# A Hymba-style layer on one core: token chunks of 272, 384, 384 instead of 352, 344, 344, and a reordered first stage

## The chip, the core and the metric

The kernel runs on one core of one Trainium2 chip. The metric is device time in microseconds (us). The core has a matrix engine (TensorE, PE in the profile, with its weight loads shown apart as PEld), a vector engine (VectorE, DVE), an activation engine (ScalarE, ACT), a general one (GpSimd, POOL) and a queue engine (SyncE, SP). Each works through its own instructions in order. DMAs are issued here from SP and from POOL.

## The reference

One decoder layer on 1024 tokens of width 1024, float32, with 16 learned meta tokens set in front, so 1040 rows in all. The parts, each with a residual and an RMSNorm ahead of it:

```
h = h + 1/2 * SwiGLU_1(RMSNorm(h))          # 1024 -> 2 x 2816 -> 1024
u = RMSNorm(h) @ W_in                       # 1024 -> 3584
o = concat[ HGRN2(u_hgrn), StickBreaking(u_sb) ]
h = h + o @ W_out
h = h + 1/2 * SwiGLU_2(RMSNorm(h))
swiglu(h) = (silu(h @ w_gate) * (h @ w_up)) @ w_out
```

HGRN2 is a gated linear recurrence with 4 heads of 128, stick-breaking attention has 8 heads of 64. The meta tokens are dropped at the end.

## The kernel before, in words

Every product is made of three matmuls on rounded float32 operands: each operand is split into a high part, cast by ACT, and a low part, the rest, made by a DVE subtraction; high x high, low x high and high x low are summed in PSUM (`times`, lines 316 to 323, order wh.xh, wl.xh, wh.xl).

The tokens of the first feed-forward layer are cut into three chunks, `THIRDS` (line 29): chunk 0 with n0 columns, chunks 1 and 2 with nw columns each. Chunk 0 is multiplied plainly. Chunks 1 and 2 go together through a Strassen-like scheme: with the pair of chunks as one side and two halves of the inner dimension as the other, seven block products stand in for eight. The operands of the seven products are called B11, B21, B22, T1, T2, T3, T4 and are sums and differences of the normalized chunks; `first_block` (line 665) turns a chunk's rows into columns on PE and evicts them, `first_combined` (line 681) makes the sums.

**First stage, gate and up projections** (`fast_in`, line 262). The 2816 hidden features are 22 tiles of 128, for gate and for up. It opens with chunk 0 alone: `plain_quad` (line 332) multiplies 256 features of gate or up, 48 matmuls, with four weight blocks of 256 KB (`block`, line 282: a ring called `raw`, 6 buffers, loaded from SP). Six such calls are made ahead, for six feature tiles of gate and of up. They are the time in which the rows of chunks 2 and 1 are normalized (`norm_rows`, line 638), turned and combined. Then come 22 quads (`quad`, line 339) of 84 matmuls on the pair of chunks; the last 16 of them carry also chunk 0, 48 matmuls more, with the same weights. `operand` (line 275) splits a weight block, 512 columns, in three buffers each for the high and the low part. Results go to DRAM from POOL's queue (`act1D`).

**Order in the opening** (lines 1378 to 1397). PE's order is as written by hand; the other engines' order is found by the compiler's list scheduler from the order of writing, the priorities and estimated times. Written order: all row loads (chunk 0 from SP in line 1364, chunks 2 and 1 from POOL in line 1365, nine buffers of 4 KB per partition); norm and turning of chunk 0; plain call 1; norm of chunk 2; plain call 2; norm of chunk 1; turning of chunk 2; plain calls 3 and 4; turning of chunk 1; then calls 5 and 6 with four steps of `first_combined` ahead of each; the other twelve steps; the 22 quads.

**Second stage, down projection** (`fast_out`, line 489). `plain_round` (line 544) does chunk 0 for all 22 hidden tiles f: 24 matmuls for each f, from two weight blocks of 256 KB (`raw`, line 504) and one activation tile (`right`, line 509). Both rings have `ring_bufs` buffers, 5 so far; the split parts have four buffers each (`halved`, line 514), which is two f for the weights. Behind the matmuls of f = 3 the residual `hT`, eight loads of 520 KB, is written into SP's order (`load_h`). It waits until the memory under it is free. Then seven steps follow (A12, A11, S1, S2, S4, S3, A22), each of 11 rounds of 12 matmuls, for the pair of chunks. `A11` loads 11 weight blocks of 256 KB into a place of their own (`ak`, line 527), so that these loads have no ring to wait for. The norm of the next layer is woven in between (`norm_steps`, by chunk).

After that: the projections for the mixer (`project`, `project_early` and `hgrn_fill`; the keys, values and gates of all 1040 rows go by `THIRDS`, 16 column tiles of 24 matmuls for each chunk, the rest by halves of 512), the two kinds of heads woven together (`weave`, `braid`: lists of steps with estimated costs, 0.42 ns per column and 13 ns per matmul), the output projection, and the second feed-forward layer with two chunks of 512, all Strassen.

Memory for a stage's tiles is stacked by pool. The first stage's pools are, from the bottom: the operands (X for chunk 0, then B11, B21, B22, T1, T2, T3, T4), then `w1` (raw, wh, wl, s), then the small ones. The second stage puts from the same bottom: `xh` and `xl` (33,280 bytes per partition each), the norm's tiles, `hT` (33,280 bytes), then `sk` and `ak`.

Of the kernel before, what the change touches and what calls it, by code (L numbers as in the profile page):

```python
# [11 lines left out]
F32 = mybir.dt.float32  # L12
# [3 lines left out]
AF = mybir.ActivationFunctionType  # L16
# [4 lines left out]
P = 128  # L21
D = 1024
# [5 lines left out]
EPS = 1e-6  # L28
THIRDS = [(0, 352), (352, 344), (696, 344)]
HALVES = [(META, 512), (META + 512, 512)]  # L30
# [9 lines left out]
class Block:  # L40
# [221 lines left out]
    def fast_in(self, ops, n, w_in, actD, openers, ev0, open_ev, feed=None, plain=None,  # L262
# [6 lines left out]
        nc = self.nc  # L269
        wp, pin = self.wq, self.pin  # L270
# [11 lines left out]
        def block(i, h, col):  # L282
            t = wp.tile([P, 4, P], F32, tag="raw", name="raw", bufs=6)
            nc.sync.dma_start(
                t, w_in[512 * h : 512 * h + 512, col + P * i : col + P * i + P]
                .rearrange("(k p) f -> p k f", p=P)
            )
            return t
# [200 lines left out]
    def fast_out(self, hT, cs, n, w_out, actD, load_h, ready, between=lambda a, q: None,  # L489
# [4 lines left out]
        nc = self.nc  # L494
        op, ring, pout = self.op, self.ring, self.pout
# [8 lines left out]
        def raw(i, j, q):  # L504
            t = ring.tile([P, 512], F32, tag="raw", name="raw", bufs=self.ring_bufs)
            nc.sync.dma_start(t, block(i, j, q))
            return t

        def right(key, n):
            t = ring.tile([P, n], F32, tag="act", name="act", bufs=self.ring_bufs)  # L510
            nc.sync.dma_start(t, actD[key])
            return t
# [125 lines left out]
    def norm_rows(self, ci, rows, junk):  # L638

        nc = self.nc  # L640
        for i, (row, at, m) in enumerate(rows):
# [5 lines left out]
            else:  # L647
                nc.scalar.activation(junk[0][:m], row[:m], AF.Square, accum_out=s)
            nc.scalar.activation(r, s, AF.Sqrt, bias=self.eps[:m], scale=1.0 / D)
            nc.vector.reciprocal(r, r)  # L650
# [675 lines left out]
    def run(self):  # L1326
        nc, tc, a = self.nc, self.tc, self.a
# [19 lines left out]
        with ExitStack() as c0:  # L1347
            with ExitStack() as c1:
                with tc.manual_schedule(engines={nc.tensor.engine}), ExitStack() as c2:
# [8 lines left out]
                    self.pin = self.pool("pin1", 1, PSUM, c2)  # L1358
                    self.t_bufs = 2
                    c3 = ExitStack()  # L1360
                    rp = self.pool("rows", ctx=c3, side="right")
                    junk = [rp.tile([P, D], (BF16, U8)[i], name=f"junk{i}") for i in range(2)]
                    self.row_bufs = 9
                    rows = [self.rows_of(0, rp, nc.sync)]
                    rows += [self.rows_of(ci, rp, nc.gpsimd) for ci in (2, 1)]
                    turning = []
# [14 lines left out]
                    with tc.high_priority():  # L1381
                        self.first_plain(rows[0], junk, plain)
                    next(steps)
                    self.norm_rows(2, rows[1], junk)
                    next(steps)
                    self.norm_rows(1, rows[2], junk)
                    ba = self.first_block(2, rows[1], rp, "ba", ops)
                    next(steps)
                    next(steps)
                    bb = self.first_block(1, rows[2], rp, "bb", None)  # L1390
                    made = self.first_combined(ba, bb, ops, rp, nw)
                    for _ in range(2):
                        for _ in range(4):
                            next(made)
                        next(steps)
# [6 lines left out]
                with tc.manual_schedule(engines={nc.tensor.engine}), ExitStack() as c2:  # L1402
# [8 lines left out]
                    hT = ph.tile([P, KT, T], F32, name="hT")  # L1411
                    self.ring_bufs = 5
                    early_w = []
# [155 lines left out]
            with tc.manual_schedule(engines={nc.tensor.engine}), ExitStack() as cx:  # L1569
# [71 lines left out]
                self.pin = self.pool("pin2", 1, PSUM, cx)  # L1641
                self.t_bufs = 2
                ppb = self.pool("ppb", 1, PSUM, pre)
# [18 lines left out]
            with tc.manual_schedule(engines={nc.tensor.engine}), ExitStack() as c1:  # L1662
# [16 lines left out]

                self.ring_bufs = 6  # L1680
                self.fast_out(hT, (cA, cB), n, a["ffn2_w_out"][0], actD, load_h, ready)
# [23 lines left out]
```

## Time and profile before

| | |
|---|---|
| median of 3 runs (lowest, highest) | 2140.38 us (2135.32, 2140.86) |
| the profiled execution's own time | 2136.56 us |
| its span, first to last instruction | 2134.9 us |
| PE busy | 2049.6 us, 96% |
| DVE busy | 1358.4 us, 64% |
| ACT busy | 899.1 us, 42% |
| POOL busy | 673.5 us, 32% |

Reading it: a row of the timeline gives start and length in us, engine, line, operation, output tile, input tiles, shape and how many were merged; the bracket is the idle time of the engine ahead of it and what ended it. A row with a q behind the engine's name is an instruction of the queue, so a DMA's issue. A table by windows gives for each stretch the busy time of each engine with the number of instructions, the granted clock, the share of time of the 16 DMA engines and the rate. Matmuls overlap, so a matmul's own length (the mean in a table of groups) is longer than the distance from one start to the next; how long a chain takes is read from that distance.

### The profile page before, as it was taken

To read this page: it belongs to the slowest core of one execution; us is meant where nothing else is said; L and a number is where in the kernel's file an instruction comes from. 1 tells how busy PE (TensorE), PEld (TensorE's weight loads), DVE (VectorE), ACT (ScalarE), POOL (GpSimd) and SP (SyncE) were. 2 spreads that over 40 slices of the span, in tenths; PEclk is the share of its full clock that TensorE was granted. 3 is DMA by queue.
4 is the path that set the end of the run, shared out by engine and by line. 5 is a ranking of instruction groups with operands and counts; after the bars stand their busy time and mean duration, and the time that the engine had idled before them with its cause. 6 is when DMAs were issued, how large, how long until landed. Compare 5 with 4: busy or idle time off the path is not lost. (4 is left out here: it accounts for less than half of the span.)

```text
span 2134.9 us, 32078 instructions
## 1 busy us (share of the span) xinstructions
PE 2049.6 (96%) x11520; PEld 1841.8 (86%) x11520; DVE 1358.4 (64%) x2072; ACT 899.1 (42%) x1859; POOL 673.5 (32%) x732
## 2 busy tenths in 40 slices
PE   6899999999999999999999999999899999999998
PEld 6899999999999989988887878877688888878887
DVE  5775544555589843246666757658767677676774
ACT  7543333333465633455565623335223333234443
POOL 2265544452000322333443400112545454440000
PEclk9999999999999999999999999999999999999999
DMA  6543333324867735434444171334533333358363
GB/s 178 163 153 118 121 105 102 103 92 174 263 197 227 228 93 160 145 129 114 117 138 113 59 262 49 97 114 123 173 104 109 94 109 99 104 180 278 104 202 133
DMA packets 271311, 300.19 MB, mean 141 GB/s; under 512 B 24784, under 2 KB 197904, under 8 KB 271152
## 3 DMA queue, kind: packets, MB, share of 16 engines
q1 hardware_dynamic: 252656, 244.88, 38.0%
q0 software_dynamic: 17456, 53.26, 6.8%
q8 instruction: 91, 1.49, 0.3%
q14 instruction: 68, 0.56, 0.1%
q10 hardware_dynamic: 1040, 0.00, 0.0%
HBM read 215.96 MB, written 82.11 MB: 140 GB/s over the span
## 5 line engine op out<-in xcount | busy, mean ns | idle before, releaser
L320 PE MATMUL qb<-T,wh 128*128 128x344 f32 (+1 forms) x1056 | 312.4, 358 | 11.0 <-DVE u L362 7.1
L279 DVE TENSOR_TENSOR wl<-s,wh 128x512 fp32r<-128x512 f32 x176 | 203.5, 1157 | 115.1 <-ACT wh L277 112.2
L320 PEld LDWEIGHTS qb<-T,wh 128*128 128x128 f32 x1056 | 194.0, 190 | 36.0 <-ACT wh L277 8.8
L588 PE MATMUL o<-tl,wh 128*128 128x344 f32 (+1 forms) x616 | 219.2, 357 | 3.4 <-DVE tl L518 3.3
L588 PE MATMUL o<-th,wh 128*128 128x344 f32 (+1 forms) x616 | 219.2, 357 | 3.3 <-DVE hT L598 3.3
L588 PE MATMUL o<-th,wl 128*128 128x344 f32 (+1 forms) x616 | 218.9, 357 | 0.7 <-DVE wl L518 0.7
L320 PE MATMUL qa<-B,wh 128*128 128x344 f32 (+1 forms) x704 | 210.4, 363 | 0.0
L163 PE MATMUL proj<-xh,wh 128*128 128x344 f32 (+2 forms) x576 | 208.0, 361 | 0.9 <-ACT xh L1443 0.9
L277 ACT CAST wh<-s 128x512 fp32r<-128x512 f32 x176 | 109.4, 622 | 225.9 <-PE qb L320 158.3
L279 DVE TENSOR_TENSOR wl<-raw,wh 128x512 fp32r<-128x512 f32 x172 | 151.0, 881 | 81.1 <-ACT wh L277 77.5
L164 PE MATMUL proj<-xh,wl 128*128 128x344 f32 (+2 forms) x576 | 202.1, 351 | 0.0
L165 PE MATMUL proj<-xl,wh 128*128 128x344 f32 (+2 forms) x576 | 201.7, 350 | 0.2 <-POOL xl L1444 0.2
L277 ACT CAST wh<-raw 128x512 fp32r<-128x512 f32 x172 | 106.0, 620 | 200.7 <-PE qc L320 98.3
L320 PE MATMUL qb<-T,wl 128*128 128x344 f32 (+1 forms) x528 | 188.8, 358 | 0.0
L320 PE MATMUL qd<-X,wh 128*128 128x352 f32 x704 | 181.2, 325 | 0.7 <-DVE X L661 0.7
L516 ACT CAST th<-act 128x512 fp32r<-128x512 f32 (+2 forms) x176 | 95.3, 542 | 183.0 <-PE o L588 129.9
L292 POOL TENSOR_TENSOR s<-raw 128x512 f32<-128x512 f32 x88 | 120.5, 1370 | 103.7 <-DVE wl L279 69.8
L518 DVE TENSOR_TENSOR tl<-act,th 128x512 fp32r<-128x512 f32 (+2 forms) x176 | 109.9, 627 | 67.0 <-ACT th L516 66.9
L320 PEld LDWEIGHTS qa<-B,wh 128*128 128x128 f32 x704 | 129.6, 190 | 16.1
L1212 POOL TENSOR_TENSOR sig<-sig,keep 128x144 f32<-128x144 f32 (+3 forms) x64 | 92.0, 1437 | 146.2 <-DVE keep L1209 86.2
L588 PEld LDWEIGHTS o<-tl,wh 128*128 128x128 f32 x616 | 117.0, 190 | 17.1 <-DVE tl L518 4.8
L320 PE MATMUL qa<-B,wl 128*128 128x344 f32 (+1 forms) x352 | 127.0, 361 | 3.9 <-DVE wl L279 3.9
(332 smaller groups left out, 4916.8 us busy)
## 6 DMA issues: line engine op xcount, KB each, us to landing
raw<-in_ffn_w_in_dram SPq DMA_DIRECT2D x208, 256.0 KB, 3.1
raw<-in_ffn_w_out_dram SPq DMA_DIRECT2D x176, 256.0 KB, 4.0
raw<-in_w_in_dram SPq DMA_DIRECT2D x28, 512.0 KB, 4.2
ks<-kD SPq DMA_DIRECT2D x32, 260.0 KB, 5.3
ak<-in_ffn_w_out_dram SPq DMA_DIRECT2D x22, 256.0 KB, 4.6
hT<-xD SPq DMA_DIRECT2D x8, 520.0 KB, 8.7
xD<-xts POOLq DMA_DIRECT2D x16, 256.0 KB, 2.8
vD<-vhl SPq DMA_DIRECT2D x8, 512.0 KB, 4.7
```

What stands on the lines that cost most here:

```text
L163: nc.tensor.matmul(ps, wh[:, s], xs, start=k == 0, stop=False)
L164: nc.tensor.matmul(ps, wl[:, s], xs, start=False, stop=False)
L165: nc.tensor.matmul(ps, wh[:, s], xl[:, k, c0 : c0 + n], start=False, stop=k == nk - 1)
L277: nc.scalar.copy(hi, src)
L279: nc.vector.tensor_sub(lo, src, hi.bitcast(F32))
L292: op(t, x, y)
L320: nc.tensor.matmul(ps, a[:, k, :], b[:, k0 + k, :], start=start and k == 0 and i == 0, stop=k == 3 and i == 2, skip_group_check=True,)
L516: nc.scalar.copy(hi, src)
L518: nc.vector.tensor_sub(lo, src, hi.bitcast(F32))
L588: nc.tensor.matmul(banks[bank][m], y[:, m * P : (m + 1) * P], z, start=start and q == 0 and e == 0, stop=q == nq - 1 and e == 2, skip_grou ...
L1212: nc.gpsimd.tensor_mul(sig, sig, keep[:, 1 : nk + 1])
```

## The change

Four things, all in the first feed-forward layer:

1. The chunks are 272, 384, 384 columns.
2. The rows of chunks 2 and 1 are loaded from SP, not POOL, and are written into the order where they are needed: chunk 2 behind the second plain call, chunk 1 behind the third. The rows have 7 buffers, not 9. The weight ring of the first stage has 7 buffers, not 6.
3. The norm keeps its last square root of chunk 0 as `self.root`, and the first plain call is written inside `issue_after(self.root.ins)`: instructions of that call on ACT are placed behind that square root.
4. Plain calls 1 and 2 stand ahead of the norm and turning of chunk 2, call 3 ahead of the load, norm and turning of chunk 1, and calls 4, 5 and 6 follow, each behind four steps of `first_combined`; eight steps are left for the end.

And the activation ring of the second stage has 4 buffers, not 5 (`ring_bufs` is a pair now: weights, activations). The last layer keeps 6 and 6.

```diff
-THIRDS = [(0, 352), (352, 344), (696, 344)]
+THIRDS = ((0, 272), (272, 384), (656, 384))
...
-            t = wp.tile([P, 4, P], F32, tag="raw", name="raw", bufs=6)
+            t = wp.tile([P, 4, P], F32, tag="raw", name="raw", bufs=self.in_bufs)
...
-            t = ring.tile([P, 512], F32, tag="raw", name="raw", bufs=self.ring_bufs)
+            t = ring.tile([P, 512], F32, tag="raw", name="raw", bufs=self.ring_bufs[0])
...
-            t = ring.tile([P, n], F32, tag="act", name="act", bufs=self.ring_bufs)
+            t = ring.tile([P, n], F32, tag="act", name="act", bufs=self.ring_bufs[1])
...
-            nc.scalar.activation(r, s, AF.Sqrt, bias=self.eps[:m], scale=1.0 / D)
+            self.root = nc.scalar.activation(
+                r, s, AF.Sqrt, bias=self.eps[:m], scale=1.0 / D
+            )
...
-                    self.t_bufs = 2
+                    self.t_bufs, self.in_bufs = 2, 7
...
-                    self.row_bufs = 9
+                    self.row_bufs = 7
                     rows = [self.rows_of(0, rp, nc.sync)]
-                    rows += [self.rows_of(ci, rp, nc.gpsimd) for ci in (2, 1)]
...
                     with tc.high_priority():
                         self.first_plain(rows[0], junk, plain)
+                    with tc.issue_after(self.root.ins):
+                        next(steps)
                     next(steps)
+                    rows.append(self.rows_of(2, rp, nc.sync))
                     self.norm_rows(2, rows[1], junk)
-                    next(steps)
-                    self.norm_rows(1, rows[2], junk)
                     ba = self.first_block(2, rows[1], rp, "ba", ops)
                     next(steps)
-                    next(steps)
+                    rows.append(self.rows_of(1, rp, nc.sync))
+                    self.norm_rows(1, rows[2], junk)
                     bb = self.first_block(1, rows[2], rp, "bb", None)
                     made = self.first_combined(ba, bb, ops, rp, nw)
-                    for _ in range(2):
+                    for _ in range(3):
                         for _ in range(4):
                             next(made)
                         next(steps)
...
-                    self.ring_bufs = 5
+                    self.ring_bufs = 5, 4
```

More of the change, by code (lines that the diff above doesn't have):

```diff
@@ L1641, in run @@
                 self.pin = self.pool("pin2", 1, PSUM, cx)
-                self.t_bufs = 2
+                self.t_bufs, self.in_bufs = 2, 6
                 ppb = self.pool("ppb", 1, PSUM, pre)
@@ L1678, in load_h @@
                             nc.sync.dma_start(hT[:, m, c : c + n], self.h2D[m, :, c : c + n])
-                self.ring_bufs = 6
+                self.ring_bufs = 6, 6
                 self.fast_out(hT, (cA, cB), n, a["ffn2_w_out"][0], actD, load_h, ready)
```

## The prediction

> **What bounds the kernel now.** First the page, for whose time it is:
>
> ```profile
> span 2134.9 us, 32078 instructions
> PE 2049.6 (96%) x11520; PEld 1841.8 (86%) x11520; DVE 1358.4 (64%) x2072; ACT 899.1 (42%) x1859; POOL 673.5 (32%) x732
> ```
>
> PE is the bound on the average, so the change is worth what it takes off PE's work and off PE's waits. Where the waits are is in the table by windows:
>
> ```profile
> core 0: us, PE busy (x) PEld busy (x) DVE busy (x) ACT busy (x) POOL busy (x), PEclk, DMA share, GB/s
> 0.00:20.00 20.00, 3.65 (x16) 3.27 (x16) 5.57 (x17) 6.79 (x13) 5.54 (x14) 1.00 0.95 282
> 20.00:40.00 20.00, 18.80 (x106) 18.20 (x107) 16.42 (x48) 19.46 (x36) 4.24 (x7) 1.00 0.56 126
> 60.00:80.00 20.00, 18.28 (x118) 17.26 (x117) 19.62 (x38) 15.46 (x36) 4.43 (x4) 1.00 0.39 110
> 80.00:100.00 20.00, 16.29 (x87) 16.00 (x86) 12.77 (x21) 6.75 (x13) 6.72 (x7) 0.83 0.63 192
> ...
> 22.00:84.00 62.00, 54.87 (x337) 52.48 (x337) 50.59 (x118) 50.90 (x102) 13.31 (x20) 1.00 0.44 119
> ...
> 540.00:560.00 20.00, 20.00 (x128) 20.00 (x127) 9.55 (x16) 8.76 (x16) 0.00 (x0) 1.00 0.99 339
> ...
> 1700.00:1720.00 20.00, 20.00 (x89) 16.38 (x88) 13.57 (x16) 5.24 (x9) 9.90 (x11) 1.00 0.34 106
> ...
> 940.00:1240.00 300.00, 286.14 (x1763) 246.44 (x1763) 199.42 (x269) 179.34 (x456) 117.92 (x146) 0.97 0.39 107
> ```
>
> In the first 20 us PE works 3.65 us while the DMA engines are full. From 20 to 84 us ACT and DVE are nearly as busy as PE (50.9 and 50.6 of 62 us), and DVE is full at the end of it. At 80 us there is a stall, and the granted clock falls to 0.83 in that window. From 540 on PE is full, and so is the DMA. Then the timeline of the opening, for what releases PE:
>
> ```profile
> 1.44 3.37 POOL L608 DMA_DIRECT2D row<-in_x_dram  x6
> 2.66 18.44 SPq L284 DMA_DIRECT2D raw<-in_ffn_w_in_dram  x9
> 9.31 3.65 PE L631 MATMUL xps<-ident,row 128*128 128x128 f32 x16 [9.31 <-DVE ss_x L650]
> 9.88 1.06 ACT L648 ACTIVATE junk<-row 96x1024 bf16<-96x1024 f32 x1 [1.01 <-DMA row<-in_x_dram]
> 16.32 0.62 ACT L277 CAST wh<-raw 128x512 fp32r<-128x512 f32 x1 [5.29 <-DMA raw<-in_ffn_w_in_dram]
> 16.84 0.29 ACT L649 ACTIVATE ss_x<-ss_x,eps 96x1 f32<-96x1 f32 x1
> 20.16 1.54 PE L631 MATMUL xps<-ident,row 96*128 96x96 f32 x8 [7.20 <-DVE row L651]
> 20.62 3.66 ACT L660 ACTIVATE X<-xps,g 128x352 fp32r<-128x352 f32 x8
> 22.40 0.66 PE L320 MATMUL qd<-X,wh 128*128 128x352 f32 x1 [0.70 <-DVE X L661]
> 84.53 0.66 PE L320 MATMUL qa<-B,wl 128*128 128x344 f32 x1 [3.71 <-DVE wl L279]
> ```
>
> The third row tile's square root (16.84) stands on ACT behind a weight cast (16.32) that waits 5.29 us for its block; that block was issued at 2.66 and shared the DMA with six row loads from POOL. PE waits 7.20 us for it. The first real matmul is at 22.40, the first quad gets going at 84.53.
>
> **The change: PE's work.** Distances from start to start come from full windows: 20 us / 126 = 0.159 us for 352 columns (128 records less two cut at the edges), 20 / 88 = 0.227 for 512. That is 0.0128 us + 0.42 ns per column. It gives 0.126 for 272, 0.157 for 344, 0.174 for 384. Does it hold as low as 272? The nearest rows are 264 wide, in the mixer:
>
> ```profile
> 992.45 0.28 PE L1199 MATMUL z<-ks,qs 128*128 128x264 f32 x1
> 992.57 0.28 PE L1200 MATMUL z<-ks,qs 128*128 128x264 f32 x1
> 992.70 0.28 PE L1140 MATMUL oacc<-wu,v 128*128 128x256 f32 x1
> ```
>
> They start 0.12 and 0.13 apart, so it does. Counts, from the loops: at n0 44 x 24 = 1056 in the first stage, 22 x 24 = 528 in the plain round, 16 x 24 = 384 projections, 1968 in all; at nw 22 x 84 = 1848, 7 x 11 x 12 = 924 and 768, 3540 in all. Change: 1968 x (-33.5 ns) + 3540 x (+16.8 ns) = -65.9 + 59.3 = -6.6 us. Of this, the opening's 288 matmuls give -9.6; all that follows gives +3.0 (the plain round -17.7, the seven steps +15.5, the rest +5.2).
>
> **The start.** Row loads from POOL are gone from the front (six issues, 3.37 us, off POOL; six on SP, at most as long by that row, behind weight loads that are not yet wanted). Chunk 0 is now 128 + 128 + 16 rows. Taking the rows' arrival as before at worst, row tile 2 comes by 9.9, its square 1.06 and its root 0.3 end by 11.5, and its scaling by 12.5. PE turns the first two tiles until 12.96, as now, then the third by about 13.2. From the first X eviction to the first matmul it took 22.40 - 20.62 = 1.8 us. So PE starts at 14 to 15 (13 if the rows come sooner); I take 14. The first cast no longer stands in front of the root, and with 3 MB less ahead of it its block is there.
>
> **The opening until the first quad.** PE's own work is 288 x 0.126 = 36.3 plus two turnings of about 4.5 and a cold start of 1: the first quad could come at 61. But DVE has 50.6 us of work between 22 and 84. What its widths do:
>
> ```profile
> L279 DVE TENSOR_TENSOR wl<-raw,wh 128x512 fp32r<-128x512 f32 x24 | 16.0, 689 | 6.9 <-ACT wh L277 6.7
> ...
> L223 DVE TENSOR_TENSOR T<-bb,T 128x344 fp32r<-128x344 f32 x4 | 1.8, 509 | 0.0
> ```
>
> (689 - 509) / 168 = 1.07 ns per column: 44 operations that widen by 40 columns cost +1.9 us, 14 that narrow by 80 save 1.2. So 51.3 us of DVE, and ACT the same. Packed as tightly as in 60 to 80 (0.98) it ends 52.3 us after 14, at 66; packed as loosely as over the whole (0.82) at 77. The combining starts a call earlier, and eight of its steps, not twelve, are left behind the last call, which makes for the tighter end. I take 72: 12.5 us sooner than 84.53, bounds 7.5 and 18. Of it 9.6 is the narrower matmul, the rest is the start. The first quad still starts out of a wait, with a cold clock as now. The loads: chunk 2's rows are behind eight weight blocks, of which the eighth waits for the first's buffer, free by about 13; they land by 19 at the 282 GB/s of the first window and are wanted by 27. Chunk 1's stand behind four more blocks, out at about 20, landed by 26, wanted by 37: hidden.
>
> **One queue or two.** The first weight cast waited until 16.32 for a block issued at 2.66. The Trainium skill, "DMA: Bandwidth & Descriptors", section "Issuing engines are not separate DMA queues", says that DMAs of all issuing engines share the same 16 engines and interleave, and that a second issuing engine saves only issue time. By that rule moving loads to SP buys nothing in rate; what can gain is the order, and the trace agrees: the blocks were issued early and landed after the rows.
>
> **The plain round** shrinks from 84 to 67 us, and the loads in it don't:
>
> ```profile
> 513.36 3.91 SPq L1418 DMA_DIRECT2D hT<-xD  x8
> 517.38 15.36 SPq L506 DMA_DIRECT2D raw<-in_ffn_w_out_dram  x6
> 531.71 0.43 PE L554 MATMUL o<-th,wh 128*128 128x352 f32 x1 [0.81 <-ACT wh L516]
> 532.43 0.43 PE L554 MATMUL o<-th,wl 128*128 128x352 f32 x1 [0.29 <-DVE wl L518]
> ```
>
> and, from the waits of SP's queue:
>
> ```profile
> SPq L1418 <- PE qd L320: 5.9, 1, 5.9
> ```
>
> The eight loads of 520 KB wait for PE's last matmul of the first stage, so PE begins the round as they are issued. The weights behind them are split and used 18.3 us later, at 531.71. Until then PE lives on the 4.5 f in hand (five buffers and four split ones, two for each f: 4.5 x 24 x 0.159 = 17.2 us), then waits 0.81 and 0.29 us. At 272 columns 4.5 f last 13.6 us. What saves it, if anything, is memory: `hT` ends, from the bottom, at 66,560 + 16,192 + 33,280 = 116,032 bytes now, inside wh, which PE reads to the end (weights begin at 99,584, six raw blocks end at 111,872). After, it ends at 117,312, and seven raw blocks end at 117,760, so of what PE reads it needs only T3 and T4, and T4 is done 12 x (0.126 + 0.174 + 0.126) = 5.1 us before the end. Then the weights come 13.2 us after the start, and PE waits as little as now or some 2 us, as it uses them faster: +1.0. If the wait stays, it is 18.3 - 13.6 = 5 us, 6 with the second block, and a cold window. Four activation buffers and four split ones are eight f: nothing.
>
> **Elsewhere.** Wider tiles give PE 10.8% longer per step and DVE 40 columns, so these waits should not grow:
>
> ```profile
> PE qb L320 <- DVE u L362: 7.1, 5, 2.2
> PE o L588 <- DVE hT L598: 3.3, 1, 3.3
> PE flip L1066 <- DVE wm L1178: 7.7, 5, 2.0
> ```
>
> I take -1 for the first, 0 for the second, +0.5 for chunk 2's norm ahead of its early projections, 0 for the third, bounds -4 and +4, as the mixer's order shifts with the pieces.
>
> **Sum.** -12.5 + 3.0 + 1.0 - 1 + 0.5 + 0.5 for SP's longer list = -8.5 us. The profiled execution took 2136.56 us, so 2128; it was 3.8 under the median of 2140.38, which by the same step becomes 2132.
>
> **Rivals.**
>
> - *The residual's loads stay late.* Memory is not what holds them, and PE idles 6 us at f = 4. That is long enough for a cold spell: after the 3.71 us at 84.53 the window's mean clock of 0.83 is 2 x 0.17 x 20 = 6.8 us at half, 3.4 lost. Together 6 + 3.4 - 1.1 as now - 1.0 booked: +7, so 2139. For it: the SP row above. Against: the layout. The Trainium skill, "TensorE: Matmul & The Clock Gate", Part 1, says that an idle window of about 3.4 us halves PE's clock; the trace agrees at 84 us, and at 7.20 us nothing was warm to lose.
> - *DVE and ACT are the opening's bound*, already in chunk 2's part: ACT was busy 19.46 of 20 us there. Norm, casts and evictions are squeezed into fewer microseconds, PE stops in several places and turns cold each time. Then the first quad comes at 80 or so: -4.5 + 3 + 1 = 0, so 2140.
> - *The opening runs tight*, first quad at 66, the mixer a little better: -18 + 3 + 1 - 2, so 2124.
> - *Slower: the mixer's weave.* Its steps, now 272 and 384 wide, fill PE between attention jobs by estimated costs. In 940 to 1240 PE is idle 13.9 us, partly on waits like the third row above, and the clock of 0.97 loses 9 more. If the coarser fill makes both 1.8 times as long, +18, so 2150; it is slower than 2146.8 from 1.65 times on. For it: nothing orders by the real time. Against: the total of the fill is the same.
>
> **How the numbers follow.** The sum 0.54 (2132, own range 2126 to 2137); residual late 0.13; opening bound by DVE and ACT 0.13; tight 0.10; mixer 0.10. About 0.3% (6.4 us) is what a measurement of this kernel tells from none. The sum's range lies beyond that on two thirds, the tight case wholly: faster 0.46. Same 0.43, from the rest of the sum, the late loads and the bound opening. Slower 0.11, the mixer and a little of the late loads. The range for 8 in 10 reaches from the tight case less some of the mixer's 4 us to the two cases near 2140 with those 4 us and the median's own spread on them: 2119 to 2146; the slower case and the worst of the late loads are left out.
>
> **What would show it.** First qd matmul at 13 to 15, no cast ahead of the third root on ACT; first quad at 66 to 77, with DVE full before it; distances of 0.126 and 0.174 in full windows; the `hT` issues some 5 us ahead of the plain round's first matmul, and a wait of 1 to 2 us at f = 4; the seven steps full. It is wrong if PE waits for rows in the opening, if `hT` still waits for the last qd, or if 940 to 1560 grows.

## The result, and the profile after

The changed kernel takes 2124.71 us (median of 4 runs, 2121.37 to 2125.84), beside 2139.73 us for the kernel before (2135.32 to 2140.86): a ratio of 0.9931, 95% interval 0.9913 to 0.9949. Measured once more beside the experiments on another chip it took 2126.82 against 2137.69, ratio 0.9948 (0.9937 to 0.9960). So the change makes it 11 to 15 us faster; the forecast was 2132 us, 8.5 us faster. The profiled execution took 2125.84 us, 10.7 less than the one before.

The page of the profile after gives the span and the busy times of the engines:

```profile
span 2124.1 us, 32084 instructions
PE 2046.2 (96%) x11520; PEld 1836.2 (86%) x11520; DVE 1358.5 (64%) x2072; ACT 902.3 (42%) x1858; POOL 674.3 (32%) x726
```

Then the table by windows of the kernel after, with the same columns as before:

```profile
core 0: us, PE busy (x) PEld busy (x) DVE busy (x) ACT busy (x) POOL busy (x), PEclk, DMA share, GB/s
0.00:20.00 20.00, 10.01 (x54) 9.60 (x55) 11.49 (x34) 11.49 (x24) 5.90 (x11) 1.00 0.94 263
20.00:40.00 20.00, 16.53 (x114) 15.31 (x113) 15.94 (x45) 18.28 (x39) 6.65 (x12) 0.91 0.78 202
40.00:60.00 20.00, 15.15 (x103) 13.92 (x101) 16.84 (x36) 18.62 (x37) 1.09 (x2) 0.90 0.28 80
60.00:80.00 20.00, 18.60 (x114) 18.11 (x115) 16.44 (x27) 11.71 (x22) 5.58 (x5) 0.85 0.55 156
80.00:100.00 20.00, 20.00 (x118) 19.97 (x118) 11.89 (x17) 8.19 (x15) 10.27 (x8) 1.00 0.66 202
540.00:560.00 20.00, 20.00 (x160) 20.00 (x160) 12.15 (x21) 10.33 (x20) 0.00 (x0) 1.00 0.98 330
940.00:1240.00 300.00, 288.17 (x1776) 248.55 (x1775) 194.83 (x265) 173.99 (x441) 114.87 (x138) 0.98 0.38 105
```

PE does 10.01 us of work in the first 20 instead of 3.65. Between 20 and 40 us it is less busy than before (16.53 against 18.80), and from 20 to 80 its granted clock is 0.91, 0.90 and 0.85, where the windows from 20 and from 60 had 1.00. From 80 to 100 it is full: the stall and the cold window that stood there before are gone. At 540 the window holds 160 matmuls; less two cut at the edges, as the prediction counts, one starts every 20 / 158 = 0.127 us (0.126 was forecast). The timeline of the kernel after has these rows for the prediction's steps:

```profile
9.69 0.29 ACT L649 ACTIVATE ss_x<-ss_x,eps 16x1 f32<-16x1 f32 x1
9.89 1.64 ACT L277 CAST wh<-raw 128x512 fp32r<-128x512 f32 x3
12.96 3.13 ACT L662 ACTIVATE X<-xps,g 128x272 fp32r<-128x272 f32 x8 [1.43 <-PE xps L631]
14.61 0.59 PE L320 MATMUL qd<-X,wh 128*128 128x272 f32 x1 [0.93 <-DVE X L663]
76.77 0.44 PE L320 MATMUL qa<-B,wl 128*128 128x384 f32 x1 [1.00 <-DVE wl L279]
501.40 4.35 SPq L1421 DMA_DIRECT2D hT<-xD  x8
```

The third root (9.69) is now ahead of the weight casts (9.89), and the first qd matmul is at 14.61. The first quad gets going at 76.77, out of a wait of 1.00 us, not 3.71. The eight hT loads start to be issued at 501.40, 4.9 us ahead of the plain round's first matmul at 506.29.

Stage by stage, from the starts of the first matmul of each stage in the two profiled executions, with the terms of the forecast put into the same stages:

| stage | before, us | after, us | difference | forecast |
|---|---|---|---|---|
| to the first qd matmul | 22.40 | 14.61 | -7.8 | -8.4 |
| from there to the first quad | 62.13 | 62.16 | 0.0 | -4.1 |
| quads, to the plain round | 428.59 | 429.52 | +0.9 | +4.2 |
| plain round | 86.10 | 67.75 | -18.4 | -16.7 |
| seven steps and projections, to the mixer's first z | 340.53 | 355.91 | +15.4 | +16.0 |
| mixer's z part | 284.37 | 284.26 | -0.1 | 0 |
| rest | 910.74 | 909.90 | -0.8 | +0.5 |
| sum | 2134.9 | 2124.1 | -10.8 | -8.5 |

The sum is near the forecast, but the 62 us from the first qd to the first quad did not shrink at all, though 288 matmuls in them became 33 ns shorter each.

### The profile page after: what moved, and what is told of

It is laid out like the page before. It is cut to its first block, busy times and chain, and to the rows that moved or that the text cites. A ratio compares the mean times of both kernels' runs of the same rounds, so it can differ in the third digit from the quotient of the medians.

```text
span 2124.1 us, 32084 instructions
## 1 busy us (share of the span) xinstructions
PE 2046.2 (96%) x11520; PEld 1836.2 (86%) x11520; DVE 1358.5 (64%) x2072; ACT 902.3 (42%) x1858; POOL 674.3 (32%) x726
## 4 chain that ended last, share of the span: by engine, by line
PE 45%; DVE 4%; issue 1%; DMA 1%; ACT 1%; SPq 0%; POOL 0%; DVEq 0%; ACTq 0%
PE o L588 10%; PE qb L320 8%; PE qc L320 6%; PE qa L320 5%; PE lvl L837 2%; PE proj L163 2%; PE proj L165 2%; PE proj L164 2%; PE wo L164 1%; PE wo L163 1%; PE wo L165 1%; PE flip L1068 1%; PE oacc L1142 1%; DMA QA<-hg_q 1%; PE oacc L1144 1%
## 5 line engine op out<-in xcount | busy, mean ns | idle before, releaser
L320 PE MATMUL qb<-T,wh 128*128 128x384 f32 (+1 forms) x1056 | 321.4, 365 | 8.8 <-DVE u L362 4.9
L588 PE MATMUL o<-tl,wh 128*128 128x384 f32 (+1 forms) x616 | 223.7, 365 | 2.9 <-DVE tl L518 2.9
L588 PE MATMUL o<-th,wl 128*128 128x384 f32 (+1 forms) x616 | 223.5, 364 | 2.0 <-DVE wl L518 2.0
L588 PE MATMUL o<-th,wh 128*128 128x384 f32 (+1 forms) x616 | 223.7, 365 | 0.3 <-DVE hT L598 0.3
L320 PE MATMUL qa<-B,wh 128*128 128x384 f32 (+1 forms) x704 | 215.2, 368 | 0.0
L163 PE MATMUL proj<-xh,wh 128*128 128x384 f32 (+2 forms) x576 | 207.4, 360 | 1.0 <-ACT xh L1446 1.0
L165 PE MATMUL proj<-xl,wh 128*128 128x384 f32 (+2 forms) x576 | 201.3, 349 | 0.5 <-POOL xl L1447 0.5
L164 PE MATMUL proj<-xh,wl 128*128 128x384 f32 (+2 forms) x576 | 201.4, 350 | 0.0
L320 PE MATMUL qb<-T,wl 128*128 128x384 f32 (+1 forms) x528 | 192.9, 365 | 0.0
L320 PE MATMUL qd<-X,wh 128*128 128x272 f32 x704 | 150.3, 298 | 0.9 <-DVE X L663 0.9
```

The source lines that it names most:

```text
L163: nc.tensor.matmul(ps, wh[:, s], xs, start=k == 0, stop=False)
L164: nc.tensor.matmul(ps, wl[:, s], xs, start=False, stop=False)
L165: nc.tensor.matmul(ps, wh[:, s], xl[:, k, c0 : c0 + n], start=False, stop=k == nk - 1)
L320: nc.tensor.matmul(ps, a[:, k, :], b[:, k0 + k, :], start=start and k == 0 and i == 0, stop=k == 3 and i == 2, skip_group_check=True,)
L588: nc.tensor.matmul(banks[bank][m], y[:, m * P : (m + 1) * P], z, start=start and q == 0 and e == 0, stop=q == nq - 1 and e == 2, skip_grou ...
```

## The experiments

The first theory was the prediction's second rival in a milder form: ACT and DVE have about 51 us of work in the opening, and that sets its length, so the narrower matmuls earn nothing there. If so, the gain belongs to the new order and queue, and the widths cost 3 us.

**The parts of the change, one at a time.** The new opening at the old widths:

```diff
-THIRDS = ((0, 272), (272, 384), (656, 384))
+THIRDS = [(0, 352), (352, 344), (696, 344)]
```

> The new opening (one queue, order of need, last chunk turned behind the third quad, seven weight blocks) at the old widths 352, 344, 344. Theory A, ACT and DVE set the opening's length: their work is the same at either width (51.4 and 52.0 us between the first qd matmul and the first quad after the change, 51 before), so the first quad starts at 76 to 79 again, with PE in fewer stops, and the total is 6 to 11 us under the kernel before. Theory B, PE sets it: 288 matmuls at 0.159 instead of 0.126 us put the first quad at 86, and the total is 0 to 2 us over the kernel before. Either way the first qd matmul is at 14 to 16, the plain round takes 84 to 87 us, and the hT loads wait for PE's last qd matmul, since hT reaches 116,032 bytes up and seven weight blocks end at 113,920.

Measured: 2120.92 us, ratio 0.9923 (0.9904 to 0.9942). That is 17 us under the kernel before, measured beside it (2137.91), more than the 6 to 11 expected. The first qd is at 14.86, the first quad at 74.63, sooner than expected and sooner than in the profiled execution with the narrow widths (76.77), with 9.6 us more work for PE. The plain round takes 84.48. The hT loads wait for the last qc matmul, not for qd, which is 1.7 us ahead of the round; that part of the expectation was wrong. No PE wait in the round came of it.

The new widths in the old opening (before, with seven row buffers):

```diff
-THIRDS = [(0, 352), (352, 344), (696, 344)]
+THIRDS = ((0, 272), (272, 384), (656, 384))
-                    self.row_bufs = 9
+                    self.row_bufs = 7
```

> The old opening and queues with the new widths 272, 384, 384 (seven row buffers instead of nine, as the wider blocks leave no room). Theory: the widths alone gain little. First qd matmul at 21 to 23; first quad at 80 to 86, since ACT and DVE, not PE, set the opening; hT overlaps the weights that PE reads to the end, so its loads wait for the last qd, PE waits 4 to 6 us at f = 4 of the plain round and loses 3.4 more to a cold clock. Total between 0 and +8 us over the kernel before. Rival, matmul counts decide: -6.6 us.

Measured: 2139.60 us, ratio 1.0015 (1.0000 to 1.0031): no gain, possibly a small loss. The first qd is at 19.53, sooner than the expected 21 to 23, the first quad at 82.43. PE waits 3.2 us at f = 4, less than the 4 to 6 expected, and the plain round takes 71.96 us.

Because the difference between the widths is small, the new opening with either width was measured again, side by side:

> The changed kernel once more, unedited, beside the next run on the same chip: 2121 to 2126 us.

> The new opening at the old widths once more. Theory (the new widths cost 3.0 us of PE's work behind the opening, and their 9.6 us in the opening are lost to waits and a cold clock, because ACT and DVE set its length): 2 to 6 us under the unedited changed kernel beside it, first quad no later than there, and no cold window before the first quad. Rival (the widths gain their 6.6 us): 5 to 8 us over it.

Measured: 2126.82 us (ratio 0.9948, 0.9937 to 0.9960) with the new widths, 2124.28 us (0.9938, 0.9923 to 0.9953) with the old. From the first quad to the first z the traces show 853.2 and 854.0 us with the new widths and 849.6 and 851.8 with the old, 1.4 to 4.4 less. The sign is the same in both measurements and in the traces and the size is near the forecast's +3.0, but the intervals overlap. What is shown is that the widths earn nothing; that they cost 3 us is likely, not shown. One part of the expectation failed: at the old widths there was one cold window of 3.41 us before the first quad in this execution, and the first quad (76.25) was later than in the one beside it (74.43).

The old order of the opening with the new widths, one queue and seven blocks:

```diff
-                    next(steps)
                     rows.append(self.rows_of(2, rp, nc.sync))
                     self.norm_rows(2, rows[1], junk)
-                    ba = self.first_block(2, rows[1], rp, "ba", ops)
                     next(steps)
                     rows.append(self.rows_of(1, rp, nc.sync))
                     self.norm_rows(1, rows[2], junk)
+                    ba = self.first_block(2, rows[1], rp, "ba", ops)
+                    next(steps)
+                    next(steps)
                     bb = self.first_block(1, rows[2], rp, "bb", None)
...
-                    for _ in range(3):
+                    for _ in range(2):
```

> After, with the old order of the opening (both norms ahead of their chunks' turnings, last chunk turned behind the fourth block of weights, two calls of combining ahead of the last weights), the loads still on one queue and held behind the root. Theory (the order is worth something of its own, since PE has more weights in hand while the combining runs): first qd unchanged at 14 to 16, first quad 3 to 7 us later at 80 to 84, total 3 to 7 us over after. Rival (only the start matters): first quad within 1.5 us of 76.8, total within 1.5 us of after.

Measured: 2135.12 us, ratio 0.9997 (0.9986 to 1.0008). First qd at 14.95, first quad at 81.88. The order is worth 8.3 us beside the unedited kernel on the same chip. The early start is lost in two places. One is the norm ahead of the weight casts. In ACT's and PE's timeline of this run:

```profile
19.08 1.28 ACT L395 ACT_TABLE_LOAD   x1
20.37 0.40 ACT L395 ACTIVATE sp<-qd 128x272 f32<-128x272 f32 x1
20.79 1.28 ACT L649 ACT_TABLE_LOAD   x1
22.08 0.29 ACT L649 ACTIVATE ss_x<-ss_x,eps 128x1 f32<-128x1 f32 x1
22.39 1.28 ACT L395 ACT_TABLE_LOAD   x1
...
24.10 1.28 ACT L649 ACT_TABLE_LOAD   x1
```

```profile
27.29 0.60 PE L320 MATMUL qd<-X,wh 128*128 128x272 f32 x1 [4.53 <-ACT wh L277]
81.88 0.69 PE L320 MATMUL qa<-B,wl 128*128 128x384 f32 x1 [6.23 <-DVE wl L279]
```

Roots and SiLUs take turns on ACT with a table load of 1.28 us between them, and PE waits 4.53 us for a weight cast behind them. The other place is the combining, below.

The old queues with the new order: rows of both later chunks on POOL's queue from the start, weights not held behind the root:

```diff
                     rows = [self.rows_of(0, rp, nc.sync)]
+                    rows += [self.rows_of(ci, rp, nc.gpsimd) for ci in (2, 1)]
...
-                    with tc.issue_after(self.root.ins):
-                        next(steps)
+                    next(steps)
                     next(steps)
-                    rows.append(self.rows_of(2, rp, nc.sync))
...
-                    rows.append(self.rows_of(1, rp, nc.sync))
```

> After, with the rows of the second and third chunk on POOL's queue from the start and the weights not held behind the root, as in the kernel before; new order, new widths, seven blocks of weights. Theory (the queues set the start and, in the new order, the start is passed on to the first quad): first qd at 18 to 22 as the first blocks land behind the rows, first quad at 80 to 84, total 4 to 7 us over after (2129 to 2132). Rival (ACT and DVE make up a late start, as where the old order got 0.5 us at the first quad from a start 4.6 us sooner): first qd later but first quad within 1.5 us of 74 to 77, total within 2 us of after.

Measured: 2132.88 us, ratio 0.9984 (0.9969 to 0.9998). First qd at 19.60, first quad at 81.96. The start, 5.0 us later than in the profiled execution after, is passed on whole: the first quad is 5.2 us later. ACT's timeline shows why it is late:

```profile
13.83 0.62 ACT L277 CAST wh<-raw 128x512 fp32r<-128x512 f32 x1 [2.36 <-DMA raw<-in_ffn_w_in_dram]
14.35 0.29 ACT L649 ACTIVATE ss_x<-ss_x,eps 16x1 f32<-16x1 f32 x1
```

Here too the root stands behind a cast that waits for its block. The hold behind the root went together with the queue; which of the two brings the early start was not tried. So with seven blocks and the new widths the order alone brings the ratio to 0.9984, the queue with the hold alone to 0.9997, and all together to 0.9931 and 0.9948: where one of the two is missing, most of the other's gain is missing too.

**The seventh weight block.**

```diff
-                    self.t_bufs, self.in_bufs = 2, 7
+                    self.t_bufs, self.in_bufs = 2, 6
```

> After, with six weight blocks in the first stage instead of seven: hT now reaches past the raw blocks into wh, which PE reads to its last qd matmul. Theory (memory decides when the residual comes): the hT loads wait for PE's last qd and are issued at the plain round's start instead of 5 us ahead, PE waits 4 to 6 us at f = 4 and turns cold, the plain round takes 72 to 77 us instead of 67.7, and the total is 5 to 9 us over after (2130 to 2134). Rival: the DMA has room, the loads catch up, and the total stays within 1.5 us of after.

Measured: 2133.66 us, ratio 0.9986 (0.9975 to 0.9997). The timeline of this run has

```profile
506.90 3.73 SPq L1421 DMA_DIRECT2D hT<-xD  x8
525.20 0.39 PE L554 MATMUL o<-th,wh 128*128 128x272 f32 x1 [2.91 <-ACT wh L516]
525.93 0.39 PE L554 MATMUL o<-th,wl 128*128 128x272 f32 x1 [0.33 <-DVE wl L518]
```

and PE's waits in the plain round of the unedited kernel are

```profile
PE o L554 <- DVE wl L518: 0.3, 1, 0.3
PE o L554 <- DVE sp L398: 0.2, 1, 0.2
```

The loads are issued 1.3 us ahead of the round (508.17) instead of 4.9 (they wait for the last qc), PE waits 2.9 + 0.3 us at f = 4, and the round takes 70.37 us instead of 67.75. So memory does decide when the residual comes. The wait is smaller than expected, and no cold window followed. The medians differ by 7 to 9 us and the profiled executions by 3.9; 2.6 us of the 3.9 lie in the round, and the round itself begins 1.9 us later, as the edit also takes a weight buffer from the opening. Where the rest of the medians' difference lies is not settled, since only one execution has a trace, and it was this kernel's fastest. The smaller activation ring (four buffers, not five) was not tried alone.

**What sets the opening.** Less work for ACT: one root for the three row tiles of a chunk.

```diff
+            if ci:
+                continue
             self.root = nc.scalar.activation(
...
+        if ci:
+            s, r = (self.ss[:, 3 * ci : 3 * ci + 3, x] for x in (0, 1))
+            nc.scalar.activation(r, s, AF.Sqrt, bias=self.eps, scale=1.0 / D)
+            nc.vector.reciprocal(r, r)
+            for i, (row, at, m) in enumerate(rows):
+                nc.vector.tensor_scalar_mul(row, row, r[:, i : i + 1])
```

> After, with one square root and one reciprocal per chunk for the second and third chunk instead of three each, so that ACT changes its table less often. Theory A (the amount of ACT's work sets the opening): ACT loses four roots (1.2 us) and two to four table loads (2.6 to 5.1 us) of its 51.4, the first quad starts 2 to 5 us sooner, and the total is 2 to 5 us under after (2120 to 2123). Theory B (what sets it is the place of the weight casts in ACT's and DVE's queues, behind batches of operand work): the first quad moves by less than 1 us, or comes later, as the first scaling waits for all three squares.

Measured: 2122.03 us, ratio 0.9942 (0.9922 to 0.9962), between the two of the unedited kernel. The table loads did not get fewer (seven in the opening, as before), ACT was 0.9 us less busy, and the first quad came at 74.87. Undecided. A plainer test leaves the norm of both later chunks out:

```diff
-                    self.norm_rows(2, rows[1], junk)
...
-                    self.norm_rows(1, rows[2], junk)
```

> After, with the norm of the second and third chunk left out (six squares, roots and scalings; its output is not the reference's). PE's instructions are those of after. Theory A (ACT's and DVE's work sets the opening): ACT loses about 12 us (six squares of 1.05, six roots of 0.3, some table loads of 1.28), DVE about 8 (six scalings of 0.75, six reciprocals, two squares of 1.2), the first quad comes 6 to 10 us sooner, at 65 to 70, and the total is 6 to 12 us under after. Rival (the chain of transposes, evictions and combining sets it, or the place of the weight casts in the queues): first quad at 73 to 77, as after.

Measured: 2125.98 us, ratio 0.9946 (0.9930 to 0.9962), first quad at 73.39. With 7.7 us less of ACT's work and 6.6 less of DVE's in the opening, the first quad came 1.0 us sooner than in one execution of the unedited kernel (74.43) and 3.4 than in the other (76.77), not 6 to 10, and the ratio lies between the two of the unedited kernel. The theory that the amount of work of the two engines sets the length of the opening falls in this form. The opening has to be cut in two at the point where the combining starts (the first subtraction of `first_combined`). The windows from the first qd to that point, and from there to the first quad, first of the kernel after, then of the old widths, then without the norm:

```profile
14.61:46.70 32.09, 27.17 (x180) 25.51 (x180) 24.35 (x64) 28.65 (x56) 7.12 (x12) 0.95 0.69 197
46.70:76.77 30.07, 25.27 (x157) 24.00 (x158) 27.72 (x51) 22.70 (x46) 6.12 (x6) 0.83 0.44 126
```

```profile
14.86:46.42 31.56, 28.13 (x180) 26.65 (x180) 23.42 (x61) 30.36 (x56) 6.03 (x12) 1.00 0.72 191
46.42:74.63 28.21, 26.04 (x158) 24.40 (x158) 28.19 (x53) 22.99 (x48) 8.70 (x6) 1.00 0.38 108
```

```profile
14.82:45.37 30.55, 26.48 (x180) 25.06 (x180) 17.43 (x49) 21.19 (x41) 6.14 (x12) 0.96 0.77 220
45.37:73.39 28.02, 21.62 (x158) 19.94 (x158) 28.02 (x51) 22.41 (x45) 6.72 (x6) 0.99 0.40 114
```

In the second half DVE (the third of the busy times) is full at the old widths, 28.19 of 28.21 us, and without the norm, 28.02 of 28.02; in the profiled execution after it works 27.72 of 30.07. The same stretch of the unedited kernel's second execution, of the kernel before and of the old order:

```profile
46.41:74.43 28.02, 21.43 (x158) 19.87 (x158) 28.02 (x51) 22.51 (x46) 6.55 (x6) 0.95 0.44 127
```

```profile
61.60:84.53 22.93, 17.89 (x109) 16.74 (x110) 22.93 (x45) 15.79 (x37) 5.25 (x5) 0.98 0.39 113
```

```profile
57.62:81.88 24.26, 15.07 (x109) 13.76 (x110) 24.21 (x45) 16.89 (x37) 8.74 (x5) 0.97 0.32 92
```

It is full there too: 28.02 of 28.02, 22.93 of 22.93 and 24.21 of 24.26. It is not in every run: in seven of the thirteen executions in which DVE does the combining, all seven with the new order, it stood idle for 0.4 to 2.4 us of the stretch. In the profiled execution after, 1.04 and 0.80 us of this were waits for weight casts of ACT. And with the old queues, as in the last version below, PE came to the first quad without a wait, so there PE's work and DVE's list ended together.

From the first subtraction on, DVE has a nearly fixed list: the combining, its splits, and the weights of the calls that are still to come. The first quad's weights stand at its end. So the first quad is the time of the first subtraction plus that list and what DVE waits in it: 61.60 + 22.9 before, 57.62 + 24.3 in the old order, 46.41 + 28.0 and 46.70 + 27.7 + 2.4 in the two executions after. The new order turns the last chunk one plain call earlier and leaves one call's weights more for behind it: the subtraction comes sooner, and the list grows by six operations (51 instead of 45). PE's matmuls lie beside the list at both widths that were run: in the second execution after, PE is busy 21.43 us of the stretch, at the old widths 26.04, and the first quad comes at 74.43 and 74.63.

What PE saved shrank besides. In the profiled execution after, its busy time in the two halves is 52.4 us, at the old widths 54.2: 1.7 us less, not 9.6. PE's stops got longer (the longest 2.96 us, 1.1 at the old widths), and after a stop its matmuls came at little more than half the pace for a while (0.227 us apart behind the stop shown below, instead of 0.127), with a mean granted clock of 0.95 and 0.83 against 1.00 and 1.00.

In the first half ACT has the most work, 28.65 of 32.09 us and 30.36 of 31.56, and the 144 narrower matmuls did not shorten it. But the amount of ACT's work does not set it either: without the norm ACT is busy 21.19 us of 30.55, and the half is only 1.5 us shorter. One thing in the way there is a wait of 2.04 us, 0.74 in the kernel after, in DVE's timeline of the run without the norm:

```profile
40.05 0.16 DVE L125 TENSOR_TENSOR mx<-l,l 128x4 f32<-128x4 f32 x1 [2.04 <-DMA l<-in_hgrn_lb_logits_dram]
...
40.40 1.89 DVE L279 TENSOR_TENSOR wl<-raw,wh 128x512 fp32r<-128x512 f32 x3
```

A constant's load comes late, and three weight differences for PE stand behind it in DVE's queue. What else holds the first half there is open.

The place of PE's stop inside the list was tried as well. PE stops for 2.96 us in the kernel after. DVE's timeline ahead of the stop's end, and the first matmuls behind it in PE's:

```profile
54.90 1.96 DVE L695 TENSOR_TENSOR bb<-bb,bb 128x384 f32<-128x384 f32 x4
56.97 0.44 DVE L398 TENSOR_TENSOR sp<-qd,sp 128x272 f32<-128x272 f32 x1
57.39 1.96 DVE L223 TENSOR_TENSOR T<-bb,T 128x384 fp32r<-128x384 f32 x4
59.27 1.89 DVE L279 TENSOR_TENSOR wl<-raw,wh 128x512 fp32r<-128x512 f32 x3
```

```profile
60.01 0.59 PE L320 MATMUL qd<-X,wl 128*128 128x272 f32 x1 [2.96 <-DVE wl L279]
60.40 0.65 PE L320 MATMUL qd<-X,wh 128*128 128x272 f32 x2
60.86 0.43 PE L320 MATMUL qd<-X,wl 128*128 128x272 f32 x1
61.08 0.65 PE L320 MATMUL qd<-X,wh 128*128 128x272 f32 x2
```

Eight operations of combining (and one of an activation, L398) stand ahead of the weight difference that PE needs. Behind the stop three matmuls take 61.08 - 60.40 = 0.68 us. With the weights ahead of each four steps:

```diff
                     for _ in range(3):
+                        next(steps)
                         for _ in range(4):
                             next(made)
-                        next(steps)
```

> After, with each of the last three blocks of weights split ahead of four steps of combining, not behind them. Theory (PE's stop of 3 us at 56.8 is a matter of place: the weights' casts and differences stand behind four steps of operand work in ACT's and DVE's queues): that stop and its cold window of 6.83 us at half clock go, the first quad comes 2 to 6 us sooner, total 2 to 6 us under after. Rival (the work is the same, so the stop moves to the combining, which then ends later): first quad within 1.5 us of 76.8.

Measured: 2126.27 us, ratio 0.9949 (0.9930 to 0.9968), first quad at 75.58. The stop at 56.8 is gone, and PE stops before the first quad instead (1.9 and 2.5 us in its first matmuls). The list is as long (28.22 us of 29.52), and the first quad is within the rival's 1.5 us of 76.8 (1.2 us later than in the second execution after), so the rival is right: the stop only moves.

Subtractions of the combining on POOL (twelve were meant):

```diff
         t2 = []
+        nc, sub = self.nc, self.nc.gpsimd.tensor_sub
         for j in range(4):
-            sub(b11[j], b12[j], b11[j])
+            nc.gpsimd.tensor_sub(b11[j], b12[j], b11[j])
             t2.append(pool.tile([P, n], F32, name=f"t2{j}"))
-            sub(t2[j], b22[j], b11[j])
+            nc.gpsimd.tensor_sub(t2[j], b22[j], b11[j])
```

Eight subtractions move in this loop, and the name `sub` moves the eight for T3 and T4 behind it, so it is sixteen, not twelve.

> After, with twelve of the subtractions that combine the blocks (0.55 us each, 6.6 us) on POOL instead of DVE; POOL is busy 13 us of the 62. Theory (the amount of DVE's work sets the opening, with ACT's): DVE falls to 45 us between the first qd and the first quad, which comes 3 to 6 us sooner; total 3 to 6 us under after. Rival A (ACT alone sets it, 51 us): first quad within 1.5 us of 74 to 77. Rival B (POOL takes 1.1 to 1.2 us for each, going by 1.45 us for 512 columns, and they are a chain, so the splits wait for them): first quad 2 to 8 us later.

Measured: 2133.88 us, ratio 0.9983 (0.9972 to 0.9994), first quad at 84.25, 7.5 us later than in the profiled execution after, and 9.8 later than in the second one: rival B, whose bound was 8. Rows of the groups of this run, then the same split in the kernel after (columns: busy us, mean ns, idle before):

```profile
L690 POOL TENSOR_TENSOR ba<-bb,ba 128x384 f32<-128x384 f32 x4 | 4.7, 1202 | 9.0 <-ACT bb L675 9.0
L223 DVE TENSOR_TENSOR T<-bb,T 128x384 fp32r<-128x384 f32 x4 | 5.2, 1351 | 0.0
```

```profile
L223 DVE TENSOR_TENSOR T<-bb,T 128x384 fp32r<-128x384 f32 x4 | 2.0, 554 | 0.0
```

POOL takes 1.20 us where DVE took 0.55, and DVE's own splits beside it take 1.35 instead of 0.55. The Trainium skill, "SBUF — State Buffer", section "Who interferes with whom", says that DVE and GpSimd share one pair of ports as an exclusive lock; the trace agrees, as DVE's operation of 0.55 us becomes about as long as one of POOL's. From POOL's first subtraction (45.27) to the first quad DVE was busy 27.24 of 38.98 us, with sixteen operations fewer. So DVE's list got no shorter and had waits in it besides, and it isn't shown by intervention that a shorter one would bring the first quad forward. That DVE is full through the stretch, to within 0.05 us, is what six of the thirteen executions show: before, the old order, the new widths in the old opening, the old widths, no norm, and the second one after.

**A version to beat both.** The new opening at the old widths, and the first two row tiles of a chunk sharing a root:

```diff
-THIRDS = ((0, 272), (272, 384), (656, 384))
+THIRDS = [(0, 352), (352, 344), (696, 344)]
...
+            if ci and i == 0:
+                continue
+            if ci and i == 1:
+                s, r = (self.ss[:, 3 * ci : 3 * ci + 2, x] for x in (0, 1))
             self.root = nc.scalar.activation(
...
+            if ci and i == 1:
+                nc.vector.tensor_scalar_mul(rows[0][0], rows[0][0], r[:, 0:1])
+                r = r[:, 1:2]
```

> The new opening at the old widths, with the first two row tiles of the second and third chunk sharing a root and a reciprocal. By the run of the one root at the new widths (first quad 1.9 us sooner than the profiled run of after, ACT 0.9 us less busy) the first quad comes 0 to 2 us sooner than the 74.6 and 76.3 at the old widths, total 2118 to 2124, under both kernels. Rival: no difference to the old widths with all roots, 2121 to 2124.

Measured: 2124.19 us, ratio 0.9944 (0.9932 to 0.9956): no better than the old widths with all roots, first quad at 76.35. The best seen is the plain new opening at the old widths (2120.92 and 2124.28 us), ahead of the changed kernel by less than the intervals tell apart.

## Why the prediction was right and wrong

The time lies 7 us under the forecast and inside its range, and faster, which had the larger chance by a little (0.46 against 0.43). By the two profiled spans the step-by-step sum was off by 2.3 us, made of errors in both directions: up to the first quad the forecast gained 4.7 us too much, behind it 7.0 us too little. That these nearly cancel is luck.

- *PE's work.* Right: distances of 0.127 us against 0.126, the seven steps and what follows up to the mixer +15.4 against +16.0. The line through the prediction's own two distances is 7.9 ns + 0.43 ns per column, not 12.8 ns + 0.42; it makes the sum -6.8 instead of -6.6 us, so nothing hangs on it. That these numbers can be added up stage by stage was wrong for the opening alone.
- *The start.* Right: 14.61 (14 forecast), with the root ahead of the casts. The run with the old queues has it back at 19.60. The rows of chunk 1, "landed by 26", were not: the last two tiles were issued at 23.06, and ACT waited 0.82 us for one until 30.94.
- *The opening until the first quad.* Wrong, by 4.8 us: 76.77 against 72, at the loose end of 66 to 77. The step that failed is "Of it 9.6 is the narrower matmul, the rest is the start". None of it was the narrower matmul: the old widths reach the first quad at 74.63 and 76.25, the new ones at 76.77 and 74.43. It was as much as the start gained (7.8 us at both points), and it could be passed on only because the order changed with it. The prediction had DVE's amount of work nearly right (51.3 us, 52.1 measured), and then treated it as something to be packed more or less tightly around PE's work. It should have asked when DVE's last list can start, and read off that before the change DVE was full from there, 22.93 of 22.93 us, to the end. What sets the time of the first subtraction stays open. The second rival (ACT and DVE bind) had the right engines, and a price that was wrong: it put the first quad at 80.
- *"The first quad still starts out of a wait, with a cold clock as now."* Half wrong. There is a wait, of 1.00 us, but the granted clock from 80 to 100 is 1.00 where it was 0.83. The quads took +0.9 us, not +4.2; the 3.3 us between are the size of the cold window that was lost before (an estimate from that clock: 0.17 x 20 = 3.4).
- *The plain round.* The place was right (hT needs only memory that PE has left; issued 4.9 us ahead, 5.1 forecast; with six blocks a wait of 2.9 us comes). The size was off: the booked +1.0 for waits at f = 4 was not there, waits fell from 1.1 to 0.5 us, so -18.4 against -16.7.
- *Elsewhere and the mixer.* Within 1.5 us. The rival of a slower mixer fell: 288.17 us busy of 300 between 940 and 1240, 286.14 before.
- *The step to the median.* The forecast added the 3.8 us by which the old profiled execution lay under its median. The new one was the slowest of its four runs, which is chance, so in the first set of runs the gain reads 15.0 us, in the second 10.9, in the two profiles 10.7.

## What to carry to other kernels

When a stage holds more than one nearly full engine, look for the point from which one of them is full to the last, and date that point: here the stage ended there plus that engine's list and its waits, and matmul time saved beside the list brought nothing. An order and a queue that only work together showed next to nothing when either was tried alone (ratios 0.9984 and 0.9997 against 0.9931 and 0.9948), so a part that looks worthless alone isn't yet worthless. Before work is handed to an idle engine, compare what the receiver needs for it and what the giver's own operations cost beside it: 1.20 us for 0.55, and 1.35 for 0.55.

## What the runs showed of the hardware

The second execution of the unedited changed kernel, on another chip, recorded a granted clock of 0.95 almost throughout, and yet worked at the same pace. The windows from 100 to 500 us, first of this run, then of the first one:

```profile
100.00:500.00 400.00, 397.90 (x2512) 396.79 (x2512) 218.42 (x323) 140.62 (x257) 206.57 (x221) 0.95 0.35 111
```

```profile
100.00:500.00 400.00, 397.88 (x2512) 396.77 (x2511) 216.88 (x322) 141.26 (x258) 208.33 (x222) 1.00 0.36 112
```

2512 matmuls in 400 us in both. So a recorded clock a little under one, all along, was no lost time here. A stretch at little more than half the pace was: behind the stop of 2.96 us three matmuls took 0.68 us, where three at 0.127 take 0.38. The recorded clock can also miss such a stretch: the first qd matmuls of the kernel after are as slow, three in 0.68 us, and the window from 0 to 20 records 1.00.

```profile
15.22 0.65 PE L320 MATMUL qd<-X,wh 128*128 128x272 f32 x2
15.68 0.43 PE L320 MATMUL qd<-X,wl 128*128 128x272 f32 x1
15.90 0.65 PE L320 MATMUL qd<-X,wh 128*128 128x272 f32 x2
```

The distance from start to start in the timeline decides.

Two profiled executions of one kernel (the new opening at the old widths) differed by 8.1 us in span, 2114.4 and 2122.5. Their mean granted clocks, 0.994 and 0.990, make about 13 and 21 us of lost time (an estimate: the missing share times the span). A difference of this size between single executions can be cold windows alone, so a few microseconds were read from stages and medians here, not from spans.
